# First norm, conditioning quarters and the order of the last product's chunks in a fused trunk step

## The chip, the cores and the metric

One core of one Trainium2 chip runs the whole kernel in one launch. The metric is device time in microseconds (us), as a median over runs; the profiled execution is one more run, taken with the profiler on. The engines are named as in the profile: PE multiplies matrices, DVE, ACT and POOL work element by element, SP only issues DMA transfers.

## The reference, cut to what matters

```python
# D_MODEL 1024; 1024 prompt tokens and 8 sequences x 8 sample tokens; DEPTH 1
sh, sc, gt = ada_mod(c, w_ada_mix, b_ada_mix)      # silu(c) @ w + b, split in three
h = rms_norm(x, norm_mix) * (1 + sc) + sh          # the start of the kernel
P = h @ w_in                                       # 30 column blocks of 128, K = 1024
...                                                # two branches, gates, w_out, residual
h = rms_norm(x, norm_mlp) * (1 + sc) + sh
x = x + gt * (square(relu(h @ w_ff1)) @ w_ff2)     # the last product
y = rms_norm(x, norm_final)                        # the end of the kernel
```

`rms_norm` divides each token by the root of the mean of its 1024 squares, and multiplies each feature by a weight. The conditioning vector c is one for the prompt and one for each of the eight sample sequences, so that shift, scale and gate have nine values for each feature.

## The kernel before, in words

Everything lies features first: a tensor of 1024 features and 1088 tokens (1024 prompt tokens, then 64 sample tokens) is eight row blocks `kb` of 128 features. Each product is done as three reduced-precision matmuls: every operand is split in a high part `hi` and a rest `lo`, and PE adds hi·hi, hi·lo and lo·hi (`mm3`, through `mm` at L148). A row block of h therefore is two tiles (the profile calls both `hx`), and a weight tile of 128x512 is loaded raw, copied to `whi` on ACT (L167) and subtracted to `wlo` on DVE or POOL (L168). The 1088 tokens are cut in three chunks of 364, 362 and 362.

The order on PE is the order in which the program is written: `Pace.run` weaves a main stream (the products) with side work by planned times. The order on the other engines is set by a scheduler from priorities and buffers.

**The start** (`start`, L342 to L410). SP loads the eight x rows (L359, 544 KB each); a small transfer on ACT's queue loads the sample columns of x once more into `smp` (L350), in pieces of 256 bytes. ACT squares each row (L362), DVE adds the squares up over the eight blocks (L366), and `stats` multiplies that sum by a column of ones, block of 128 tokens by block, so that the sums stand tokens first. `rms` (L281) takes the root on ACT, inverts on DVE, spreads the values back over 128 partitions by PE transposes (L155) and copies them to `rb` on ACT (L303). Meanwhile the conditioning weight `w_ada_mix` comes in two halves of eight tiles 128x1024 (L372); half i holds shift and scale for row blocks 4i to 4i+3. `ada_part` (L239) multiplies it in by column-tiled matmuls (eight rows of the trace for each turn of two tiles), copies the result (`asb`, L255), adds up the four column groups with a selection matrix (the eight rows `wc<-kct,asb`), adds the bias (`am`, L263), and `mod_scale` makes g (L268). Then for each row block: h = x·g·rb on DVE (L391), hi on ACT (L393), lo on DVE (L395). The sample columns go a separate way through `smp` on DVE (L386 to L388, L396). Row blocks 0 to 3 need the first half, 4 to 7 the second. The products of the first two column blocks of P start with row block 0 and go on as row blocks come; the second half's conditioning runs between them.

**The middle** is a long run of products with the recurrent branch beside it. Two small loads there are issued by SP: `plw` (L531) and the pool state (`spool`, L478).

**The end** (`last`, `norm3`, from about L1400). The last product runs through the tokens in three chunks `FCH`, of 448, 384 and 256 columns. For each of eight row blocks m, `residual` (L1448) adds the gated result to x on DVE (L1454); where the chunk holds the sample columns it needs one more DVE operation (L1457) and an addition on POOL (L1459). Squares on ACT (L1431), sums on DVE (L1433), `stats` and `rms` follow for each chunk, and then eight output rows: six on DVE (L1444), and in the last chunk two by POOL (L1441) and ACT (L1442). SP stores each row (L1445). The sample columns lie in the last chunk.

Of the kernel before, what the change touches and what calls it, by code (L numbers as in the profile page):

```python
# [18 lines left out]
P = 128  # L19
# [3 lines left out]
TS = 8  # L23
# [94 lines left out]
class K:  # L118
# [38 lines left out]
    def weights(self, src):  # L157
# [10 lines left out]
        (nc.gpsimd if n % 2 and n >= self.solo else nc.vector).tensor_tensor(lo, raw, hi.bitcast(F32), op=ALU.subtract)  # L168
# [112 lines left out]
    def rms(self, po, col, blocks, out):  # L281
# [7 lines left out]
        for i in range(0, k, 4):  # L289
            m = min(4, k - i)  # L290
            ps = self.ps("wc")
# [50 lines left out]
    def start(self, st, order):  # L342
# [4 lines left out]
        aw = lambda: st.tile([P, 1024], F32, tag="aw", bufs=8, name=self.nm("aw"))  # L347
        asb = st.tile([P, 512], F32, name="asb")
        smp = st.tile([P, 8, 64], F32, name="smp")
        nc.scalar.dma_start(smp, io["xT"][:, :, NPR:NT].rearrange("k p n -> p k n"))  # L350
        blocks = self.blocks(0, NT)
        po = self.ps("w")
        rt = self.cp.tile([P, 16], F32, tag="rt", bufs=2, name=self.nm("rt"))
        nc.scalar.activation(rt[:, 0:1], self.eps[:, 0:1], AF.Sqrt)
        xs = []
        t = None
        for kb in range(8):
            x = self.row(st, "x", 8)
            nc.sync.dma_start(x, io["xT"][kb])  # L359
            xs.append(x)  # L360
            sq = self.row(st, "sq", 3)
            nc.scalar.activation(sq, x, AF.Square)  # L362
            if t is None:
                t = sq
            else:
                nc.vector.tensor_tensor(t, t, sq, op=ALU.add)  # L366
        ws = []

        def load(i):
            for k in range(8):  # L370
                ws.append(aw())
                nc.sync.dma_start(ws[-1], io["w_ada_mix"][k, i])  # L372
# [3 lines left out]
        self.stats(po, t, blocks, True, True)  # L376
        rb = self.row(st, "rb", 1)
        pr, sa = slice(0, NPR), slice(NPR, NT)

        def part(i, gaps, turn):  # L380
            yield from self.ada_part("w_ada_mix", i, lambda: ws.pop(0), asb, self.am, "b_mix", (4 * i, 8 + 4 * i), gaps, turn)
            self.mod_scale(g, self.am, "norm_mix", 4 * i, 4 * i + 4)
            ks = slice(4 * i, 4 * i + 4)
            seq = lambda t: t[:, ks, 1:9].unsqueeze(3).to_broadcast([P, 4, 8, 8])
            s4 = smp[:, ks].rearrange("p k (q t) -> p k q t", t=TS)
# [15 lines left out]
        def rest():  # L401
            yield from part(1, (0, 0, 3000, 1500), 1500)
            self.done.add("h")
# [1174 lines left out]
```

## Time and profile before

| | |
|---|---|
| median of 3 runs | 1755.21 us (1754.6 to 1755.97) |
| profiled execution | 1759.32 us |
| its span on the core | 1757.5 us |
| PE busy | 1692.8 us (96%) |
| DVE / ACT / POOL busy | 845.0 / 546.1 / 255.1 us |
| mean granted TensorE clock | 0.984 |

The span runs from the first to the last instruction of the profiled execution; the times in the rows count from its start. A timeline row gives start, duration, engine, line, operation, output and inputs, shape, the number of instructions merged in the row, and in brackets how long the engine idled before and what released it. One fp32 matmul stands in the trace as two rows. Line numbers are those of the kernel before.

### The profile page before, as it was taken

Reading aid. Unit: us, or ns where it says so; the run is one execution under the profiler, and the core shown is the slowest. Engines: PE = TensorE matmul, PEld = TensorE weight load, DVE = VectorE, ACT = ScalarE, POOL = GpSimd, SP = SyncE. Lnnn points to the kernel's source line nnn. Section 1 sums busy time; section 2 is a strip of 40 time slices with the busy share of each in tenths; the row PEclk is TensorE's granted clock in tenths of the full one; section 3 lists DMA queues with packets and bytes.
Section 4 is the critical chain, followed back from the end, with each engine's and each line's share of the span. In section 5 each row is a group of like instructions: output and inputs, shape, how many; then the busy total and the mean of one; then the engine's idle time right before and its main releaser. Section 6 shows DMA issues by size and latency. Waiting matters only on the chain.

```text
span 1757.5 us, 32572 instructions
## 1 busy us (share of the span) xinstructions
PE 1692.8 (96%) x13705; PEld 1583.7 (90%) x13705; DVE 845.0 (48%) x1540; ACT 546.1 (31%) x1100; POOL 255.1 (15%) x335
## 2 busy tenths in 40 slices
PE   5999999999999999999999999999999999999997
PEld 2989878887888798899798999999999999999997
DVE  5577465746573744335437633323333333324346
ACT  4443343343343433322225521213121212212132
POOL 0120110000000000005314411111111111111111
PEclk9999999989999999999999999999999999999998
DMA  8233314222413241847842311111111111111112
GB/s 336 82 128 118 125 65 135 85 81 94 147 41 129 80 137 57 314 168 276 299 151 85 136 45 49 43 44 47 43 46 45 43 49 43 43 49 43 43 43 103
DMA packets 80083, 179.61 MB, mean 102 GB/s; under 512 B 16480, under 2 KB 23136, under 8 KB 79936
## 3 DMA queue, kind: packets, MB, share of 16 engines
q1 hardware_dynamic: 72128, 156.66, 26.0%
q10 hardware_dynamic: 6512, 15.96, 2.7%
q0 software_dynamic: 1296, 4.90, 0.7%
q8 instruction: 108, 1.77, 0.4%
q14 instruction: 39, 0.32, 0.1%
HBM read 138.64 MB, written 38.84 MB: 101 GB/s over the span
## 4 chain that ended last, share of the span: by engine, by line
PE 86%; DMA 4%; DVE 4%; ACT 2%; issue 2%; POOL 1%; SPq 0%; DVEq 0%; ACTq 0%; POOLq 0%
PE mm L148 58%; PE w L148 24%; PE wc L148 4%; DMA t<-d_th 1%; DMA smp<-in_xT 1%; PE w L155 1%; POOL t L1266 1%; DMA aw<-in_w_ada_mix 1%; DMA wraw<-in_w_in 1%; DMA hid<-in_w_ada_mlp 0%; ACT whi L167 0%; DVE hx L1444 0%; DMA wraw<-in_w_ff 0%; POOL wlo L168 0%; DVE wlo L168 0%
## 5 line engine op out<-in xcount | busy, mean ns | idle before, releaser
L148 PE MATMUL mm<-hx,whi 128*128 128x362 f32 (+2 forms) x2608 | 683.1, 344 | 2.6 <-ACT px L465 2.0
L148 PEld LDWEIGHTS mm<-hx,whi 128*128 128x128 f32 x2608 | 458.8, 191 | 39.6 <-issue 20.4
L148 PE MATMUL mm<-hx,wlo 128*128 128x362 f32 (+3 forms) x1304 | 430.7, 330 | 1.8 <-DVE wlo L168 1.8
L167 ACT ACTIVATE whi<-wraw 128x512 fp32r<-128x512 f32 x246 | 155.1, 630 | 531.4 <-PE w L148 359.1
L148 PE MATMUL mm<-ma,whi 128*128 128x364 f32 (+1 forms) x1280 | 318.0, 330 | 0.2 <-ACT whi L167 0.2
L148 PEld LDWEIGHTS mm<-hx,wlo 128*128 128x128 f32 x1304 | 249.9, 192 | 2.3 <-DVE wlo L168 2.1
L148 PEld LDWEIGHTS mm<-ma,whi 128*128 128x128 f32 x1280 | 226.7, 189 | 7.3 <-issue 5.0
L168 POOL TENSOR_TENSOR wlo<-wraw,whi 128x512 fp32r<-128x512 f32 x89 | 117.6, 1322 | 670.4 <-ACT whi L167 670.4
L168 DVE TENSOR_TENSOR wlo<-wraw,whi 128x512 fp32r<-128x512 f32 x157 | 110.4, 704 | 211.6 <-ACT whi L167 211.3
L148 PE MATMUL mm<-ma,wlo 128*128 128x364 f32 (+1 forms) x640 | 210.4, 329 | 0.1
L1454 DVE SCALAR_TENSOR_TENSOR hx<-mm,aq,hx 128x364 f32<-128x364 f32 (+4 forms) x136 | 74.8, 588 | 207.8 <-PE mm L148 207.5
L148 PE MATMUL w<-mb,whi 128*128 128x362 f32 x640 | 159.1, 330 | 2.5 <-DVE rs L1457 2.1
L148 PEld LDWEIGHTS mm<-ma,wlo 128*128 128x128 f32 x640 | 120.6, 189 | 0.4 <-DVE wlo L168 0.4
L148 PEld LDWEIGHTS w<-mb,whi 128*128 128x128 f32 x640 | 112.7, 189 | 5.9 <-issue 4.4
L1349 DVE TENSOR_TENSOR ft<-ft 128x362 f32<-128x362 f32 (+1 forms) x96 | 53.1, 577 | 131.5 <-ACT ft L1348 131.2
L148 PE MATMUL w<-mb,wlo 128*128 128x362 f32 x320 | 105.5, 330 | 0.8 <-DVE wlo L168 0.8
L148 PE MATMUL w<-hx,whi 128*128 128x362 f32 x416 | 103.2, 329 | 0.1
L148 PE MATMUL mm<-hid,whi 128*128 128x364 f32 (+4 forms) x304 | 75.0, 328 | 0.0
L148 PEld LDWEIGHTS w<-hx,whi 128*128 128x128 f32 x416 | 73.7, 190 | 0.4 <-DVE hx L396 0.4
L1348 ACT ACTIVATE ft<-mm 128x364 f32<-128x364 f32 x64 | 29.5, 475 | 124.9 <-PE mm L148 124.7
L148 PE MATMUL w<-hx,wlo 128*128 128x362 f32 x208 | 67.8, 326 | 0.0
L1459 POOL TENSOR_TENSOR hx<-hx,rs 128x64 f32<-128x64 f32 x72 | 38.6, 537 | 176.8 <-DVE rs L1457 176.6
(309 smaller groups left out, 2120.8 us busy)
## 6 DMA issues: line engine op xcount, KB each, us to landing
wraw<-in_w_ff SPq DMA_DIRECT2D x134, 256.0 KB, 2.6
wraw<-in_w_in SPq DMA_DIRECT2D x68, 256.0 KB, 2.8
hid<-in_w_ada_mlp SPq DMA_DIRECT2D x24, 512.0 KB, 4.8
d_th<-px SPq DMA_DIRECT2D x22, 544.0 KB, 3.0
wt<-d_x SPq DMA_DIRECT2D x20, 544.0 KB, 4.4
t<-d_th ACTq DMA_DIRECT2D x16, 544.0 KB, 5.7
aw<-in_w_ada_mix SPq DMA_DIRECT2D x16, 512.0 KB, 7.2
wraw<-in_w_out SPq DMA_DIRECT2D x32, 256.0 KB, 2.9
```

The costliest lines, as they stand in the source:

```text
L148: return self.nc.tensor.matmul(out, lhsT, rhs, **kw)
L155: self.nc.tensor.transpose(out, in_, ident)
L167: nc.scalar.activation(hi, raw, AF.Copy)
L168: (nc.gpsimd if n % 2 and n >= self.solo else nc.vector).tensor_tensor(lo, raw, hi.bitcast(F32), op=ALU.subtract)
L1266: nc.gpsimd.tensor_tensor(t, t, S["u"], op=ALU.add)
L1348: nc.scalar.activation(t[:, :n], ps[:, :n], AF.Relu)
L1349: nc.vector.tensor_tensor(t[:, :n], t[:, :n], t[:, :n], op=ALU.mult)
L1454: nc.vector.scalar_tensor_tensor(x[:, c0:c0 + m], ps[:, :m], gt[:, 0:1], x[:, c0:c0 + m], op0=ALU.mult, op1=ALU.add)
L1459: nc.gpsimd.tensor_tensor(x[:, NPR:NT], x[:, NPR:NT], t, op=ALU.add)
```

## The change

**First norm.** The squares of row blocks 0-2, 3-5 and 6-7 are added up on DVE as three groups. PE multiplies each group by a 128x128 matrix of ones, in three parts of 512, 512 and 64 tokens, which leaves the sum over all features on every partition. The root is taken from there; a 32x32 transposing on DVE, a reciprocal of one value per token, and a transposing of the spread value give `rb`. `stats`, `rms` and the load of `smp` are no longer used at the start. **Conditioning.** `w_ada_mix` is loaded in quarters, each two tiles of [128, 2, 4, 256] by two transfers each, with runs of 1 KB; quarter qi holds shift and scale for row blocks 2qi and 2qi+1. The first rows are made in three chunk pieces. The sample columns are made in place in x, on POOL. The first two `wlo` are made on POOL. **Loads.** `plw` and the pool state are issued from POOL. **End.** `FCH` is reversed, so that the sample columns lie in the first chunk; six of eight output rows of the middle chunk (`late`) are put behind the last residual, with a copy `nf` of the norm's weights that POOL makes from there; six rows of the last chunk read the spread values directly from PSUM.

```diff
+                if kb % 3:
+                    nc.vector.tensor_tensor(ts[-1][:, s], ts[-1][:, s], sq[:, s], op=ALU.add)
+            if kb % 3 == 0:
+                ts.append(sq)
+            if kb in (2, 5, 7):
+                for s, ps in zip(parts, pss):
+                    self.mm(ps[:, :s.stop - s.start], ones, ts[-1][:, s], start=kb == 2, stop=kb == 7)
...
+            for r in range(2):
+                w = st.tile([P, 2, 4, 256], F32, tag="aw", bufs=5, name=self.nm("aw"))
+                for s in range(2):
+                    o = s * 512 + qi % 2 * 256
+                    nc.sync.dma_start(w[:, s], io["w_ada_mix"][4 * r:4 * r + 4, qi // 2, :, o:o + 256].rearrange("k p c -> p k c"))
...
+            nc.scalar.activation(rb[:, s], ps[:, :n], AF.Sqrt, bias=self.eps[:, 0:1], scale=1.0 / D)
+            nc.vector.transpose(rt1[:, s], rb[:, s])
+            nc.vector.reciprocal(rr[:, c], cut32(rt1)[:, c, 0])
+            nc.vector.transpose(cut32(rb)[:, c, :], rr[:, c].unsqueeze(2).to_broadcast([P, n // 32, 32]))
...
+                xq = cut8(x[:, sa])
+                nc.gpsimd.tensor_tensor(xq, xq, g[:, kb, 1:9].unsqueeze(2).to_broadcast([P, 8, 8]), op=ALU.mult)
+                nc.gpsimd.tensor_tensor(x[:, sa], x[:, sa], rb[:, sa], op=ALU.mult)
+                nc.gpsimd.tensor_tensor(xq, xq, self.am[:, kb, 1:9].unsqueeze(2).to_broadcast([P, 8, 8]), op=ALU.add)
+                nc.scalar.activation(hi[:, sa], x[:, sa], AF.Copy)
+                nc.gpsimd.tensor_tensor(lo[:, sa], x[:, sa], hi[:, sa].bitcast(F32), op=ALU.subtract)
...
+                    late = [] if ci == 0 else [lambda m=m, out=out, r=rb[:, c0:c0 + n]: out(m, r) for m in range(2, 8)]
+                    for m in range(8 if ci == 0 else 2):
+                        out(m, rb[:, c0:c0 + n], ci == 1)
+                else:
+                    for m in (7, 6, 0, 1, 2, 3, 4, 5):
+                        out(m, rb[:, c0:c0 + n] if m > 5 else self.rps[:, :n], m > 5)
...
-FCH = [(0, 448), (448, 384), (832, 256)]
+FCH = [(640, 448), (256, 384), (0, 256)]
```

PE at the start, before: from the last transpose of the norm through the selection (`wc_292`) and the second half's first turns (`wc_342`) to the first products (`mm_354`, `w_355` are the first column block).

```order
13 L155 MATMUL wc_289<-kct,rt_261 128x128
14 L148 MATMUL wc_292<-kct,asb 128x18 x4
15 L148 MATMUL wc_342<-aw_326,sT 32x512 x2
16 L148 MATMUL wc_342<-aw_328,sT 32x512 x2
17 L148 MATMUL wc_342<-aw_330,sT 32x512 x2
18 L148 MATMUL wc_342<-aw_332,sT 32x512 x2
19 L148 MATMUL mm_354<-hx_147,whi_236 128x364
20 L148 MATMUL mm_354<-hx_148,whi_236 128x364
21 L148 MATMUL mm_354<-hx_147,wlo_237 128x364
```

PE at the start, after: the last of the ones products (`sq_218,ones`), quarter 0 (`wc_271`), its selection, and the first products.

```order
8 L148 MATMUL mm_180<-sq_218,ones 128x512
9 L148 MATMUL mm_181<-sq_218,ones 128x64
10 L148 MATMUL wc_271<-aw_232,sT 32x512 x4
11 L148 MATMUL wc_271<-aw_235,sT 32x512 x4
12 L148 MATMUL wc_282<-sel_173,asb_280 128x9 x4
13 L148 MATMUL mm_334<-hx_147,whi_240 128x364
14 L148 MATMUL mm_334<-hx_148,whi_240 128x364
15 L148 MATMUL mm_334<-hx_147,wlo_241 128x364
```

The half and its first turns of the next half ahead of the products are now one quarter; six turns (of four matmuls each) and three selections of the later quarters stand among the products of row blocks 0 to 4, where two turns and one selection stood.

DVE between the second quarter's selection and the lo parts of its rows, after (`hx_152` and `hx_154` are the lo parts of row blocks 2 and 3).

```order
35 L414 TENSOR_TENSOR am<-wc_372,part 128x2x18 [waits PE_49]
36 L268 SCALAR_TENSOR_TENSOR g_172<-am,part 128x18 [waits DVE_49]
37 L422 SCALAR_TENSOR_TENSOR h_379<-x_191,g_172,sq_256 128x1024 [waits DMAHW3_49,DVE_49]
38 L422 SCALAR_TENSOR_TENSOR h_388<-x_199,g_172,sq_256 128x1024 [waits DMAHW4_49]
39 L424 SCALAR_TENSOR_TENSOR hx_152<-h_379,am,hx_151 128x1024 [waits Activation_49]
40 L424 SCALAR_TENSOR_TENSOR hx_154<-h_388,am,hx_153 128x1024 [waits Activation_49]
```

Before, row blocks 2 and 3 had no selection of their own: their h stood behind the lo parts of row blocks 0 and 1.

```order
24 L395 SCALAR_TENSOR_TENSOR hx_148<-h_302,am,hx_147 128x1024 [waits Activation_49]
25 L395 SCALAR_TENSOR_TENSOR hx_150<-h_308,am,hx_149 128x1024 [waits Activation_49]
26 L396 TENSOR_TENSOR hx_148<-smp,hx_147 128x64 [waits Activation_49]
27 L396 TENSOR_TENSOR hx_150<-smp,hx_149 128x64 [waits Activation_49]
28 L391 SCALAR_TENSOR_TENSOR h_314<-x_188,g_172,rb_255 128x1024 [waits DMAHW4_49,DVE_49]
29 L391 SCALAR_TENSOR_TENSOR h_320<-x_193,g_172,rb_255 128x1024 [waits DMAHW5_49,DVE_49]
```

So a selection and two vector operations now stand ahead of every second row block.

DVE at the end, before, from the last residual (L1454) to the last output rows (L1444).

```order
1513 L1454 SCALAR_TENSOR_TENSOR hx_9168<-mm_17044,aq,hx_9168 128x192 [waits PE_49]
1514 L1457 TENSOR_TENSOR rs_17041<-mm_17024,aq 128x64 [waits Pool_49]
1515 L1457 TENSOR_TENSOR rs_17061<-mm_17044,aq 128x64 [waits Pool_49]
1516 L1433 TENSOR_TENSOR t_16983<-t_16983,t_17008 128x256 [waits Activation_49]
1517 L1433 TENSOR_TENSOR t_16983<-t_16983,t_17028 128x256 [waits DVE_49,Activation_49]
1518 L1433 TENSOR_TENSOR t_16983<-t_16983,t_17048 128x256 [waits DVE_49,Activation_49]
1519 L287 RECIPROCAL rt_17070<-rt_17070 128x2 [waits Activation_49]
1520 L1444 SCALAR_TENSOR_TENSOR hx_8703<-hx_8703,part,t_16572 128x256 [waits Activation_49]
```

DVE at the end, after, at the same place (`nf` rows are the middle chunk's late ones, `wc_17123` is the PSUM with the spread values).

```order
1512 L1479 TENSOR_TENSOR t_17031<-t_17031,t_17087 128x256 [waits DVE_49,Activation_49]
1513 L1515 SCALAR_TENSOR_TENSOR hx_9213<-mm_17083,aq,hx_9213 128x256 [waits PE_49]
1514 L1496 SCALAR_TENSOR_TENSOR hx_8876<-hx_8876,nf,t_16617 128x384 [waits Pool_49]
...
1519 L1496 SCALAR_TENSOR_TENSOR hx_9213<-hx_9213,nf,t_16617 128x384
1520 L287 RECIPROCAL rt_17120<-rt_17120 128x2 [waits Activation_49]
1521 L1496 SCALAR_TENSOR_TENSOR hx_8748<-hx_8748,part,wc_17123 128x256 [waits Activation_49]
```

The six late rows stand between the last residual and the reciprocal, and the sample operations are gone from there.

## Rows read from the trace of the kernel before

**Rows 1.** Windows: length, busy us (instructions) of PE, PEld, DVE, ACT, POOL; clock; DMA.

```profile
58.00:60.00 2.00, 2.00 (x9) 2.00 (x8) 2.00 (x3) 1.03 (x1) 0.00 (x0) 0.50 0.42 156
...
1000.00:1690.00 690.00, 690.00 (x4167) 686.79 (x4166) 244.11 (x459) 150.23 (x292) 102.28 (x114) 1.00 0.15 48
```

**Rows 2.** The chain that ended last, in order of time: its first two long pieces.

```profile
1.19 14.74 DMA smp<-in_xT
16.32 4.61 DMA aw<-in_w_ada_mix
```

**Rows 3.** Timeline of all engines from 0 to 39 us.

```profile
15.95 4.22 SPq L372 DMA_DIRECT2D aw<-in_w_ada_mix  x8
...
22.93 1.93 PE L148 MATMUL wc<-aw,sT 128*32 128x512 f32 x8
...
31.68 0.58 ACT L255 ACTIVATE asb<-wc 128x512 f32<-128x512 f32 x1
...
32.31 1.07 PE L148 MATMUL wc<-kct,asb 128*128 128x18 f32 x8 [1.22 <-ACT asb L255]
...
33.42 0.23 DVE L263 TENSOR_TENSOR am<-wc,part 128x72 f32<-128x72 f32 x1 [0.19 <-PE wc L148]
...
34.26 2.47 DVE L391 SCALAR_TENSOR_TENSOR h<-x,g,rb 128x1024 f32<-128x1024 f32 x2
...
36.99 2.47 DVE L395 SCALAR_TENSOR_TENSOR hx<-h,am,hx 128x1024 fp32r<-128x1024 f32 x2
```

**Rows 4.** Timeline of PE from 38 to 70 us.

```profile
38.59 0.33 PE L148 MATMUL mm<-hx,wlo 128*128 128x364 f32 x1
...
41.67 1.06 PE L148 MATMUL wc<-aw,sT 128*32 128x512 f32 x8
...
56.10 0.44 PE L148 MATMUL mm<-hx,wlo 128*128 128x364 f32 x1 [1.83 <-DVE wlo L168]
...
68.90 0.50 PE L148 MATMUL mm<-hx,whi 128*128 128x362 f32 x2
69.23 0.33 PE L148 MATMUL mm<-hx,wlo 128*128 128x362 f32 x1
```

**Rows 5.** DMA from 0 to 60 us: GB/s by 1.5 us, and queues (packets, MB, share of 16 engines).

```profile
GB/s 0 143 393 384 416 411 410 412 413 415 68 202 401 281 344 391 426 415 406 349 357 410 421 403 422 418 412 314 16 0 0 0 0 0 0 0 5 0 273 77
...
q1 hardware_dynamic: 5504, 14.55, 63.8%
q10 hardware_dynamic: 1184, 0.30, 2.3%
```

**Rows 6.** Groups on DVE and POOL by line and shape: busy us, mean ns.

```profile
L773 DVE STREAM_TRANSPOSE hv<-iv 128x512 f32<-128x512 f32 x4 | 4.8, 1197 | 1.3 <-ACT iv L770 1.3
...
L428 POOL COPY px<-sst 128x8 f32<-128x8 f32 x14 | 3.2, 235 | 5.9 <-DMA sst<-in_sst 5.8
```

**Rows 7.** Durations of L1459 on POOL, in ns: smallest, median, largest.

```profile
L1459 POOL TENSOR_TENSOR hx<-hx,rs x72: 311/378/2032, 933.9 to 1745.7; 128x64 f32<-128x64 f32 x72
```

**Rows 8.** Timeline of all engines from 67.5 to 71 us.

```profile
69.26 1.29 DVE L444 TENSOR_TENSOR d<-px 128x1096 f32<-128x1096 f32 x1
69.33 1.28 POOL L441 COPY ns<-px 128x8 f32<-128x8 f32 x1
```

**Rows 9.** Timeline of all engines from 1738 us to the end.

```profile
1738.70 4.33 DVE L1444 SCALAR_TENSOR_TENSOR hx<-hx,part,t 128x384 f32<-128x384 f32 x8
...
1742.92 0.87 PE L148 MATMUL mm<-hx,ma 128*128 128x256 f32 x6
...
1746.66 1.86 PE L148 MATMUL wc<-kct,t 128*128 128x2 f32 x8 [2.87 <-DVE t L1433]
...
1750.28 3.40 DVE L1444 SCALAR_TENSOR_TENSOR hx<-hx,part,t 128x256 f32<-128x256 f32 x6 [1.26 <-ACT t L303]
...
1750.39 1.82 POOL L1441 TENSOR_TENSOR hx<-hx,t 128x256 f32<-128x256 f32 x2 [4.16 <-ACT t L303]
```

**Rows 10.** Timeline of SP's queue from 1749 us: the last stores.

```profile
1750.83 4.14 SPq L1445 DMA_DIRECT2D o_y<-hx  x8
```

More of the change, by code (lines that the diff above doesn't have):

```diff
@@ L279, in stats, with rms @@
             self.mm(po[:, i:i + m], t[:, b:b + 128], self.kc("one0")[:, :m], start=first and i == 0, stop=last and i == len(blocks) - 1)
-    def rms(self, po, col, blocks, out):
+    def rms(self, po, col, blocks, out, tag="wc"):
         nc = self.nc
@@ L346, in start @@
         g = self.cp.tile([P, 8, 9], F32, name="g1")
[L347 to L352, printed above, removed]
+        sel = st.tile([P, 9], F32, name="sel4")
+        nc.gpsimd.tensor_tensor(sel, self.kc("sel")[:, 0:9], self.kc("sel")[:, 9:18], op=ALU.add)
+        ones = st.tile([P, P], F32, name="ones")
+        nc.gpsimd.memset(ones, 1.0)
         rt = self.cp.tile([P, 16], F32, tag="rt", bufs=2, name=self.nm("rt"))
-        nc.scalar.activation(rt[:, 0:1], self.eps[:, 0:1], AF.Sqrt)
-        xs = []
-        t = None
+        nc.scalar.activation(rt[:, 0:1], self.sT[:, 0, 0:1], AF.Sqrt, bias=self.eps[:, 0:1], scale=0.0)
+        parts = (slice(0, 512), slice(512, 1024), slice(1024, NT))
+        pss = [self.ps("mm") for _ in parts]
+        xs, ts = [], []
         for kb in range(8):
@@ L360, in start @@
             xs.append(x)
[L361 to L366, printed above, removed]
-        ws = []
[L369 to L372, printed above, removed]
+            sq = self.row(st, "sq", 4)
+            for s in parts if kb == 7 else (slice(0, NT),):
+                nc.scalar.activation(sq[:, s], x[:, s], AF.Square)
+                if kb % 3:
+                    nc.vector.tensor_tensor(ts[-1][:, s], ts[-1][:, s], sq[:, s], op=ALU.add)
@@ L398, in start @@
-        self.pace.run(iter(()), [part(0, (0, 3500, 0, 0), 1000), self.rms(po, 0, blocks, rb)])
-        load(1)
-        def rest():
-            yield from part(1, (0, 0, 3000, 1500), 1500)
+        load(1)
+        rb, rt1, rr = self.row(st, "sq", 4), self.row(st, "sq", 4), st.tile([P, 34], F32, name="rr")
+        for s, ps in zip(parts, pss):
+            n = s.stop - s.start
+            nc.scalar.activation(rb[:, s], ps[:, :n], AF.Sqrt, bias=self.eps[:, 0:1], scale=1.0 / D)
+            nc.vector.transpose(rt1[:, s], rb[:, s])
+            c = slice(s.start // 32, s.stop // 32)
+            nc.vector.reciprocal(rr[:, c], cut32(rt1)[:, c, 0])
+            nc.vector.transpose(cut32(rb)[:, c, :], rr[:, c].unsqueeze(2).to_broadcast([P, n // 32, 32]))
@@ L403, in rest @@
+        for r in range(2):
+            round_(0, r)
+        for _ in vectors(0, 0):
+            pass
+        rows(0)
+        load(2)
+        load(3)
+        def rest():
+            for qi in range(1, 4):
+                yield (1000, 3000, 2500)[qi - 1]
+                round_(qi, 0)
+                yield (600, 700, 1600)[qi - 1]
+                round_(qi, 1)
+                yield from vectors(qi, 1100)
+                rows(qi)
             self.done.add("h")
```

69 lines of the change are left out of this document (43 added, 26 removed).

## The prediction

> **What bounds the kernel now.** I read the windows first. From 1000 to 1690 us PE is busy in 690.00 of 690 us at a granted clock of 1.00 [rows 1], and the change leaves the order there as it was. So only the two ends, where PE waits, can give or take time. At the front the chain starts with the transfer of the sample columns, which lands at 15.93 us, and goes on with the conditioning weights [rows 2]. SP issues the weights at 15.95, just behind that landing [rows 3], and the DMA rate falls from 415 GB/s to 68 and 202 GB/s in the two slices from 15 to 18 us [rows 5]. The first vectors wait for 4.2 MB of weights: `asb` starts at 31.68 and h at 34.26 [rows 3]. The first product with a lo part starts one matmul (0.17 us) before the row at 38.59, at 38.4; the last product of the first two column blocks ends at 69.23 plus half of its row, 69.4 [rows 4]. The stretch takes 31.0 us. At the tail the last residual's products end at T = 1743.79, and the last of eight stores is issued at 1754.97, T + 11.2 [rows 9, 10].
>
> **Start, up to the first rows.** Without the sample transfer the weights follow x at once, from about 14.2 us: the full-rate slices end at 15.0 [rows 5], and the sample packets leave them. Their price: queue 10 moved 1184 packets in 2.3% of 16 x 60 us, 18.6 ns each of 256 bytes; queue 1 moved 5504 in 63.8%, 111 ns each of 2.64 KB [rows 5]. A straight line through both gives 8.7 ns and 0.0388 ns a byte, so 168 ns for a 4 KB run (what the kernel before uses) and 48 ns for 1 KB. The first quarter, 2.1 MB in runs of 1 KB, takes 2048 x 48 / 16 = 6.2 us and lands at 20.4; in 4 KB runs it would take 5.4. The smaller runs cost 0.8 us there (bounds 0 and 1.5, the line being drawn through mixed queues).
>
> [...] The rows here have 256 byte packets at 18.6 ns, more than twice their share.
>
> Behind the landing stand one turn on PE (1.0 us, half of 1.93 [rows 3]), the copy of the first whi ahead of `asb` on ACT, and then `asb` to h as before: 34.26 - 31.68, less a sample operation of 0.4 that now runs on POOL, 2.2 us [rows 3]. That puts h at 24.2. The norm is ready earlier. The last square ends at about 16.2; the nine ones products are 18 trace rows, of which the last group's end at 18.9; then come a root, and on DVE four transposes of 512 columns at up to 1.2 us [rows 6], and rb is whole at 23.7. If a transpose from a spread value cost twice that, rb would be last, at 25 to 26: the bound on that side.
>
> Six h pieces follow, at 2.47/2 for 1024 columns or 0.46 a piece, 2.75 us, then a lo piece of 0.5 [rows 3]: 27.5 us. Beside them POOL now makes the sample columns, six operations of 128x64 before their hi parts. Rows of POOL and DVE side by side show what that can cost: a POOL copy of 128x8 took 1.28 us beside a DVE operation of 1.29 [rows 8], where the same copy has a mean of 0.235 [rows 6]; and the six last rows on DVE took 3.40 us, 0.57 each for 256 columns [rows 9], where eight of 384 columns took 4.33, 0.54 each. So either side can be held. Six POOL operations at 0.311, the smallest, to 0.378, the median [rows 7], would hold DVE by 0 to 2.3 us; I take 0.9, about 0.15 each, as in those six rows. The first product with a lo part then stands at 28.4, **10 us earlier**.
>
> **Start, to the end of the two column blocks.** Most of it is given back. PE's work from there was 144 matmuls at 0.166 us [rows 4], two turns at 1.06 and a selection at 1.0, 27.0 us; the rest of 31.0 was a stall of 1.83 and the slow matmuls behind it [rows 4]. Now six turns and three selections stand in it: 23.9 + 6.4 + 3.0 = 33.3 us. What had hidden them, the time before the first rows, is gone. And each quarter's chain, from selection to first lo, stands on DVE with am and g (0.5), two h (1.2 each) and a lo (1.25), 4.2 us and up to 4.5 beside POOL, while PE has between 3.0 and 4.5 us of products left. Going through the order after, the stalls are 1.6 us at row block 2, 1.7 at 4 (two wlo stand there too) and 0.9 at 6, together 4.2; without POOL's hold 1.9. The stretch takes 37.5 us (35.2 without).
>
> **The clock.** Before the first rows PE now has almost nothing from 23.7 to 28.4 us. The row for that: after the idle 1.83 us at 56.10 [rows 4] the granted clock was 0.50, that is 1.2 GHz, from 58 to 60 [rows 1], and matmuls took twice as long for about 3 us, 1.7 us lost. I charge 1.9 (bounds 0 and 3). Sum: 28.4 + 37.5 + 1.9 = 67.8 against 69.4, a **gain of 1.6 us**.
>
> **Tail.** Before, eight middle rows of 4.33 us sit in front of the last residuals, and the sample operations on DVE and POOL lie between the last product and the stats at 1746.66 [rows 9]. After, two middle rows go by POOL, six wait behind the last residual. Residual at T + 0.1 to T + 0.5, square to T + 1.0, stats of 1.86 us [rows 9] from T + 1.5, of which the first half can run early, root to T + 3.6 at the latest. DVE is in the six late rows until T + 4.3 (from T + 1.0, behind `nf` on POOL, 6 x 0.54); reciprocal and spread to T + 5.2; rows from T + 5.25 at 0.41 each, since they read PSUM. Eight stores of 4.14 us [rows 10] then bound it: T + 9.9 against T + 11.2. **Gain 1.3 us** (0.5 to 2.3; the six late rows are what eats the rest).
>
> [...]
>
> **The middle** I take as 0 (±0.5): `plw` and the pool state are issued from POOL, which has gaps there, ahead of where they are used. Together 1.6 + 1.3 = 2.9 us; the profiled execution would go from 1759.3 to 1756.4, and the median from 1755.21 to **1752.4**.
>
> **The rivals.**
> First, the forecast, with the early start mostly given back: 0.44. Its own range is 1750 to 1754.5.
> Second, PE stays fed: POOL holds DVE little (27.5), the stretch takes 35.2, and with the same clock price the blocks end at 64.6, 4.8 earlier; with the tail 6.1, 1749.1. With a clock that holds it would be 1747. For it: DVE operations that did not suffer beside POOL, as the 1.29 us one [rows 8]. Against: the chains of 4.2 us, which do not depend on POOL. 0.30.
> Third, the slower side: the clock falls at each quarter. The mechanism is the 1.83 us stall at 56.10, after which PE ran at 1.2 GHz [rows 1, 4]. Its place is the waits for the first lo of row blocks 2, 4 and 6, its price 1.7 us each, 5.1 together, plus up to 3.4 where POOL holds DVE by 2.3 us (1.4 more in the first quarter, 2 in the others). It decides from the point where these stalls reach that 1.83 us; mine are 1.6, 1.7 and 0.9. The start then loses 3.5 to 6.9, the tail gives 1.3: +2.2 to +5.6, 1757.4 to 1760.8. 0.19, of which 0.12 over the slower bound.
> Fourth, that the change does not do what it says: the conditioning still comes late (runs of 1 KB at the rate of the 256 byte packets, 2048 x 74 / 16 = 9.5 us, and rb late too), rows at 27, and the start comes out even. The tail alone gives 1754. 0.07.
>
> **How the numbers follow.** A measurement of this kernel can tell 0.2%, 3.5 us, from no change: bounds 1751.7 and 1758.7. Of the forecast a third (0.14) falls under the lower bound, the rest within; the second rival is faster (0.30), the third slower by 0.12 and the same by 0.07, the fourth the same. Faster 0.44, same 0.44, slower 0.12. The range from 1746.5 to 1758.7 leaves out the best of the second (0.07) and the 0.12 of the third.
>
> **What would show it.** Right: the weights issued before 6 us or on x's heels, no gap in the DMA rate at 15 us; h at 24 to 25 us; the first lo product at 27.5 to 28.5; PE waits for lo of row blocks 2, 4 and 6 of 1 to 2 us; the first block pair ending near 68; a granted clock of 0.5 for some 3 us at the first products; last stores at T + 9.5 to T + 10.5. Wrong: PE without waits at the quarters and an end near 64 (second rival); a granted clock of 0.5 again after each quarter (third); h later than 26.5 (fourth); or middle products that shifted, since I priced them at nothing.

## The result, and the profile after

The changed kernel takes 1762.91 us (median of 10 runs, 1757.99 to 1768.07) against 1754.55 us for the kernel before, measured beside it: ratio 1.0046, interval 1.0032 to 1.0060. A second comparison later (e16 below) gave 1.0029, interval 1.0017 to 1.0040. The mean of the two is some 1.0037, or 6.5 us slower. I had forecast 2.9 us faster, and the range ended at 1758.7.

The page of the changed kernel opens with the span and the busy times: PE is busy 2.7 us longer than before, and the profiled execution is 4 us longer than the one of before (1761.5 against 1757.5). That is less than the medians differ: the profiled execution of the kernel before (1759.32 us) was 4.8 us slower than its median beside the changed kernel, that of the changed kernel (1763.26) only 0.35.

```profile
span 1761.5 us, 32639 instructions
PE 1695.5 (96%) x13712; PEld 1583.4 (90%) x13712; DVE 843.6 (48%) x1542; ACT 548.5 (31%) x1108; POOL 285.6 (16%) x383
```

I cut both spans at the same two points: the end of the first two column blocks, and T, the end of the last residual's products. Before: 69.4 us of start [rows 4], 1674.3 of middle (to T = 1743.8 [rows 9]) and 13.7 of tail. After: 69.5, 1679.4 and 12.6. So **the start came out even, the tail gave what it should, and the middle, which I had priced at 0, lost 5 us**.

**Start.** The DMA rates by 1.5 us answer to [rows 5]; the gap at 15 us is gone, and the quarters with runs of 1 KB come at some 348 GB/s.

```profile
GB/s 0 155 375 414 415 363 267 403 415 409 370 348 350 348 364 368 347 348 349 348 348 349 350 348 348 366 365 354 90 8 0 0 0 0 0 7 168 0 5 168
```

The timeline of the start (columns as in [rows 3]) has the ones products, the transposing, the first vectors, the first rows, and in the last row the end of the two column blocks: the last of their products runs into the row that starts at 69.35.

```profile
5.30 9.23 SPq L378 DMA_DIRECT2D aw<-in_w_ada_mix  x4
...
11.44 4.08 PE L148 MATMUL mm<-sq,ones 128*128 128x512 f32 x6 [11.44 <-DVE sq L364]
...
16.36 6.28 PE L148 MATMUL mm<-sq,ones 128*128 128x512 f32 x12 [0.85 <-DVE sq L364]
...
22.37 0.71 DVE L389 STREAM_TRANSPOSE sq<-sq 128x512 f32<-128x512 f32 x1 [3.71 <-ACT sq L387]
...
22.57 1.92 PE L148 MATMUL wc<-aw,sT 128*32 128x512 f32 x16
...
24.56 0.60 ACT L407 ACTIVATE asb<-wc 128x512 f32<-128x512 f32 x1 [0.64 <-PE wc L148]
...
27.09 3.39 DVE L422 SCALAR_TENSOR_TENSOR h<-x,g,sq 128x364 f32<-128x364 f32 x6
...
31.10 0.67 PE L148 MATMUL mm<-hx,whi 128*128 128x364 f32 x1 [1.92 <-DVE hx L424]
...
69.35 0.32 PE L148 MATMUL mm<-hx,wlo 128*128 128x362 f32 x1
```

h starts at 27.09 (before 34.26 [rows 3]) and the first lo product at 31.10 (its row is the one with 1.92 us of waiting). PE's waits between the first rows and 70 us, from its timeline; in brackets how long, and for whom:

```profile
43.32 0.44 PE L148 MATMUL mm<-hx,whi 128*128 128x364 f32 x1 [0.89 <-DVE hx L424]
54.26 0.43 PE L148 MATMUL mm<-hx,whi 128*128 128x364 f32 x1 [0.26 <-DVE hx L424]
57.80 0.43 PE L148 MATMUL mm<-hx,wlo 128*128 128x364 f32 x1 [0.41 <-DVE wlo L168]
63.48 0.44 PE L148 MATMUL mm<-hx,whi 128*128 128x364 f32 x1 [0.23 <-DVE hx L424]
```

Two windows of the same kernel (the granted clock is the third number from the end): 0.50 while the first rows come, and 1.00 from 58 to 60 us, where [rows 1] had 0.50. The prediction writes this 0.50 as 1.2 GHz; the profile gives the clock as a share of full speed alone. At 0.50 three products of 362 columns took 0.90 us (from 31.88 on), 1.2 columns a ns.

```profile
28.00:34.00 6.00, 3.57 (x13) 2.78 (x17) 5.52 (x11) 3.25 (x8) 3.23 (x6) 0.50 1.10 348
...
58.00:60.00 2.00, 2.00 (x16) 2.00 (x16) 0.87 (x3) 0.00 (x0) 0.46 (x2) 1.00 0.36 126
```

**Tail.** Rows that answer to [rows 9, 10]. T is 1748.04 + 0.87 = 1748.9; the sixteen stores are issued by 1758.84, T + 9.9; the six late rows start at T + 1.1, and the last six, which read PSUM, take 0.41 us each (0.57 before).

```profile
1745.56 13.28 SPq L1497 DMA_DIRECT2D o_y<-hx  x16
...
1748.04 0.87 PE L148 MATMUL mm<-hx,ma 128*128 128x256 f32 x6
...
1749.97 3.26 DVE L1496 SCALAR_TENSOR_TENSOR hx<-hx,nf,t 128x384 f32<-128x384 f32 x6 [0.54 <-POOL nf L1485]
...
1753.16 0.15 DVE L287 RECIPROCAL rt<-rt 128x2 f32<-128x2 f32 x1
...
1754.57 2.44 DVE L1496 SCALAR_TENSOR_TENSOR hx<-hx,part,wc 128x256 f32<-128x256 f32 x6 [1.26 <-ACT t L303]
```

**Middle.** From 70 us to T, PE's idle time is 36.0 us, against 29.8 before. Nearly all of it lies ahead of 1000 us in both. Two rows of PE's timeline after have no counterpart before:

```profile
197.21 0.60 PE L148 MATMUL mm<-hx,whi 128*128 128x362 f32 x2 [1.78 <-issue]
...
547.25 1.96 PE L148 MATMUL w<-ab,at 64*64 64x128 f32 x32 [1.67 <-ACT at L893]
```

In the first, PE waits for nothing that the profile shows. In the second it waits for a copy `at` on ACT. ACT's timeline after shows why: the two scalings of `wt`, which wait 5.93 us for a load, stand ahead of the copies `at` and `uv`.

```profile
545.18 1.39 ACT L606 ACTIVATE wt<-wt,part 128x512 f32<-128x512 f32 x2 [5.93 <-DMA wt<-d_x]
546.60 0.60 ACT L893 ACTIVATE at<-w 128x512 f32<-128x512 f32 x1
547.09 0.58 ACT L895 ACTIVATE uv<-w 64x512 f32<-64x512 f32 x1
```

Before, the copies stood first, and no line of the diff names any of them. ACT and PE there:

```profile
544.79 0.60 ACT L848 ACTIVATE at<-w 128x512 f32<-128x512 f32 x1 [3.57 <-PE w L148]
545.56 0.59 ACT L850 ACTIVATE uv<-w 64x512 f32<-64x512 f32 x1 [0.17 <-DVE uv L849]
547.16 1.39 ACT L561 ACTIVATE wt<-wt,part 128x512 f32<-128x512 f32 x2 [1.01 <-DMA wt<-d_x]
```

```profile
547.40 1.97 PE L148 MATMUL w<-ab,at 64*64 64x128 f32 x32
```

These two waits are real, but they are not where this pair of traces parts. The product behind the second one starts at 547.25 after and at 547.40 before, so that the two traces are level there, and they still are at 709 us. From 70 to 547 us PE was busy 3.0 us longer before (461.0 against 458.1), at a mean granted clock of 0.97 against 0.98, and idled as much less. The 5 us come between 709 us and 1000 us, where PE of the changed kernel idled 2.2 us more and had the lower clock, first after and then before:

```profile
700.00:1000.00 300.00, 287.80 (x2082) 265.60 (x2083) 143.64 (x232) 98.81 (x176) 90.76 (x85) 0.98 0.56 197
```

```profile
700.00:1000.00 300.00, 289.98 (x2123) 265.77 (x2122) 147.73 (x238) 100.84 (x180) 91.11 (x86) 1.00 0.57 200
```

One pair of executions can't tell which part of that belongs to the kernel and which to the run; the medians of the experiments below have to.

### The profile page after: what moved, and what is told of

It is laid out like the page before. It is cut to its first block, busy times and chain, and to the rows that moved or that the text cites. A ratio compares the mean times of both kernels' runs of the same rounds, so it can differ in the third digit from the quotient of the medians.

```text
span 1761.5 us, 32639 instructions
## 1 busy us (share of the span) xinstructions
PE 1695.5 (96%) x13712; PEld 1583.4 (90%) x13712; DVE 843.6 (48%) x1542; ACT 548.5 (31%) x1108; POOL 285.6 (16%) x383
## 3 DMA queue, kind: packets, MB, share of 16 engines
q8 instruction: 108, 1.77, 0.4%
## 4 chain that ended last, share of the span: by engine, by line
PE 85%; DVE 5%; DMA 4%; ACT 2%; issue 2%; POOL 1%; SPq 0%; ACTq 0%; DVEq 0%; POOLq 0%
PE mm L148 57%; PE w L148 24%; PE wc L148 3%; DMA t<-d_th 2%; PE w L155 1%; DMA wt<-d_x 1%; DVE h L422 0%; DMA wraw<-in_w_in 0%; POOL t L1311 0%; DMA hid<-in_w_ada_mlp 0%; DMA x<-in_xT 0%; DMA wraw<-in_w_out 0%; DVE wlo L168 0%; SPq L378 0%; ACT whi L167 0%
## 5 line engine op out<-in xcount | busy, mean ns | idle before, releaser
L1515 DVE SCALAR_TENSOR_TENSOR hx<-mm,aq,hx 128x364 f32<-128x364 f32 (+3 forms) x136 | 75.1, 588 | 206.3 <-PE mm L148 206.2
```

Of the source, the lines that this page charges most:

```text
L1515: nc.vector.scalar_tensor_tensor(x[:, c0:c0 + m], ps[:, :m], gt[:, 0:1], x[:, c0:c0 + m], op0=ALU.mult, op1=ALU.add)
```

## The experiments

Ratios are to the kernel before, with a 95% interval; the kernel before had medians of 1755.1 to 1756.6 us beside them. The letters of the theories in the expectations hold within one group of runs: e1 to e4, e5 to e8, e9 to e12, e13 to e16. A difference of 0.001 is 1.75 us.

### The parts of the change apart

e1 is the changed kernel with the two small loads issued by SP again:

```diff
-            nc.gpsimd.dma_start(ev[:, :, 0:15], self.io["spool"][:, g])
+            nc.sync.dma_start(ev[:, :, 0:15], self.io["spool"][:, g])
-            nc.gpsimd.dma_start(plw, self.io["pool_w"][:, g * 128:(g + 1) * 128])
+            nc.sync.dma_start(plw, self.io["pool_w"][:, g * 128:(g + 1) * 128])
```

> The changed kernel with the two small loads (plw and the pool state) issued from SP again, as in the kernel before. In the traces the two column blocks end at 69.5 us against 69.4, the tail gives 1.1 us, and the middle loses 5.1 us, of which 1.7 stand at 545.6 us, where ACT takes a scaling that waits for a DMA ahead of the copy that PE needs; with the loads on SP that swap is gone from the order. Theory A (the loads on POOL cost the middle, by that swap and by POOL's queue): some 4 to 5 us less than the changed kernel, about 1758, ratio 1.002. Theory B (any shift of the start moves the middle's transfers against its products, and the loads have no part in it): as the changed kernel, 1761 to 1763, ratio 1.0045.

e2 is the kernel before with only those two loads moved to POOL (the same lines the other way).

> The kernel before with nothing changed but the two small loads, issued from POOL. Theory A: 3 to 5 us slower than before, ratio 1.002 to 1.003. Theory B: no change, within 0.1%. Its order on PE, DVE and ACT is that of the kernel before, without the swap on ACT, so that only the queue's own price is seen.

e3 has the new start, with the loads on SP and the tail of the kernel before; e4 is the kernel before with the new tail only. Beside the late rows, the line that goes back in e3 and forth in e4 is

```diff
-FCH = [(0, 448), (448, 384), (832, 256)]
+FCH = [(640, 448), (256, 384), (0, 256)]
```

> The changed kernel with the old end (chunks of 448, 384, 256 from the front, old order of rows) and the loads on SP: the first norm and the conditioning alone. From the traces the two column blocks end 0.1 us later than before, so by Theory A: within 1 us of the kernel before, ratio 1.000. Theory B: the whole loss is here, 7 to 9 us, ratio 1.004 to 1.005.

> The kernel before with the new order of the last product's chunks and rows alone. All theories but one: 1.1 us faster, as the tails of the two traces differ, ratio 0.9994. A third theory (the new chunk order costs in the last product, ahead of the tail): slower, by 2 us or more.

Measured: e1 1759.6 us, 1.0018 (1.0005 to 1.0030); e2 1756.91, 1.0003 (0.9992 to 1.0014); e3 1759.48, 1.0020 (1.0008 to 1.0032); e4 1756.78, 0.9999 (0.9988 to 1.0010). Neither the tail nor the two loads alone cost anything. The new start costs 0.2% by itself. And taking the loads from POOL in the changed kernel gave back a part (by the first result; against e16 the intervals overlap). That had a reason besides the loads: the order on ACT is the old one in e1. Its rows there:

```profile
540.88 0.60 ACT L893 ACTIVATE at<-w 128x512 f32<-128x512 f32 x1 [3.62 <-PE w L148]
541.65 0.59 ACT L895 ACTIVATE uv<-w 64x512 f32<-64x512 f32 x1 [0.17 <-DVE uv L894]
542.68 1.39 ACT L606 ACTIVATE wt<-wt,part 128x512 f32<-128x512 f32 x2 [0.44 <-DMA wt<-d_x]
```

The load is the same, the scaling waits 0.44 us for it, and PE does not wait. So e1 against the changed kernel mixes two things, which e13 and e14 take apart.

### The clock held at the start

e5 is e1 with five unread fp32 products that keep PE busy while the first rows come: one of 512 columns ahead of the first turn, two behind the selection, two behind the first hi·hi (where `mm3` calls `fill` once).

```diff
+        dummy = self.ps("w")
+        def fill(k, n):
+            for _ in range(k):
+                nc.tensor.matmul(dummy[:, :n], ones, xs[0][:, :n], start=True, stop=True)
+        fill(1, 512)
...
+        fill(2, 512)
+        self.fill = fill
```

> The kernel of e1 (loads on SP) with five matmuls added whose result nobody reads, in the waits of PE between the ones products and the first products: one ahead of the first turn, two behind the selection, two behind the first hi·hi; everything else in the same order. Over all runs the mean granted clock of e1 and e3 was 0.983 to 0.984 against 0.986 of the kernel before, and at an equal clock their spans do not differ; in the traces 10.2 us at half clock lie around the first products (25.6 to 35.8) where the kernel before has 0 to 7. Theory C (the new start costs by the clock that falls in PE's waits before the first products): the clock stays at full there, the block pair ends 1 us or more earlier, mean clock back to 0.985 to 0.986, and 2 to 3 us faster than e1, about 1757. Theory D (the clock that is lost is lost elsewhere, or the first products wait for DVE anyway): as e1, 1759 to 1760, with the mean clock still near 0.983.

e6 adds a sixth, of 256 columns, ahead of the selection; with it the order on ACT is that of the changed kernel.

```diff
+            if qi == 0:
+                fill(1, 256)
```

> As e5, with a sixth such matmul (256 columns) ahead of the selection. With it the scheduler puts two scaling operations (wt), which wait for a DMA, ahead of two copies (at, uv) on ACT in the middle of the program, as it does in the changed kernel; nothing else differs from e5. Theory A1 (this swap on ACT is what the loads on POOL cost the changed kernel): 2 to 3 us slower than e5, with a wait of PE of some 1.7 us at 545 us, ahead of a product of ab and at. Theory A2 (POOL's queue itself costs): as e5, within 1 us.

Measured: e5 1759.17 us, 1.0020 (1.0007 to 1.0033); e6 1759.85, 1.0029 (1.0017 to 1.0040). The same window as above, first e1 and then e5:

```profile
28.00:34.00 6.00, 4.18 (x16) 2.52 (x16) 4.22 (x9) 2.09 (x6) 1.94 (x4) 0.50 1.14 313
```

```profile
28.00:34.00 6.00, 5.55 (x31) 2.38 (x29) 4.48 (x9) 2.35 (x6) 2.19 (x5) 1.00 1.14 313
```

The granted clock is 1.00 in that window of e5 (0.50 in e1), and its two column blocks end at 67.1 instead of 69.5. So the low clock at the start is real and worth 2.3 us there. Yet the whole kernel is no faster: the medians of e5 and e1 differ by 0.4 us, so that some 2 us of the gain went elsewhere. The profile of e5 has a middle 8.8 us longer than that of e1, but most of that is the choice of the execution: e5's profiled one is 3.1 us over its median, e1's is the fastest of its twelve and 3.5 us under it. It is a first hint, not more, that moving instructions costs something later on.

### The start cut out

e7 and e8 leave out all that follows the first four column blocks (outputs are then filled from loaded data); e7 has the start of before, e8 that of e1.

```diff
-        jobs += G[8:]
+        jobs = [X(0), X(8)]
...
-        self.pace.run(back, [self.chains(), self.heads(), self.pools(), self.or_rows()])
+        self.pace.run(back, [])
```

> The kernel before, cut: the start and the first four column blocks of P only; the rest of the program is left out, and the outputs are copies of one row. Its time, 110 to 130 us, is the price of the start without the noise of the rest. To be compared with e8 alone.

> The changed start (loads on SP), cut in the same way as e7. If the start itself costs the 3 us that e3 showed: 2 to 4 us slower than e7 in the medians. If the start is even, as the traces have it (block pairs end at 69.3 to 69.4 against 69.1 to 72.1): within 1 us of e7, or up to 2 us faster, and the 3 us come from the middle.

Measured: e8 121.3 to 122.4 us in four runs, mean 122.0; e7 123.08 and 124.08 us, and 126.28 and 126.35 in two more runs at a lower mean clock than the first two (0.879 against 0.891 and 0.897). The new start is 1.6 us faster by the first two, which was the forecast for it, and 3.0 by all four; so few runs that differ by 3 us are a thin base. In the profiles of the changed kernel and of the kernel before it is even.

### TensorE's instructions moved against their pieces

I took queue 8, of kind "instruction", for the one that brings PE's code. Its row on the changed kernel's page:

```profile
q8 instruction: 108, 1.77, 0.4%
```

1.77 MB in 108 packets is 16.4 KB each. The page has 2 x 13712 PE and PEld instructions; if the queue is PE's that is 64.5 bytes for each, so about 256 in a piece. That it is PE's, e15 below bears out: with 256 more PE instructions, its page shows one piece more.

```profile
q8 instruction: 109, 1.79, 0.4%
```

Around 190 us, in a burst of 32x32 products, the pieces come every 4 us. Up to the product near 195 us the traces hold 2987 instructions of PE before (matmuls, weight loads and semaphore instructions), 3010 in the changed kernel and in e1, 3009 in e3, 3031 in e5; the expectation of e11 counts to an earlier place, with the same difference of 23. The wait "issue" near 195 us is there in all of those with the higher counts, and not in before, e2 and e4. So I moved PE's instructions without touching the rest: unread products of 32x32, four PE instructions each, early in the start. The lines of e9 (6 of them, in the kernel before):

```diff
+        dummy = self.ps("w")
+        for _ in range(6):
+            nc.tensor.matmul(dummy[0:32, :32], self.kct[0:32, 0:32], self.kct[0:32, 0:32], start=True, stop=True)
```

e10 has 11, e11 is e1 with 58 (so that 23 + 232 = 255 makes a whole piece), e12 is e5 with 53.

> The kernel before with six 32x32 matmuls added whose result nobody reads, early, where PE idles; the order on all engines is else the same. They are 24 instructions of PE. In the traces PE's program comes in by 16 KB pieces on queue 8 (108 pieces for 1.77 MB, so 256 instructions of 64 bytes each), and PE stands without a named cause (issue) for 1.2 to 1.8 us at 192 to 197 us in the changed kernel, e1, e5 and e6, behind some 250 tiny matmuls, and not in the kernel before; up to there the changed kernel has 23 instructions of PE more than the kernel before, e5 45 more. Theory F (where the pieces begin in the program sets these waits, and the added instructions of the new start have shifted them): 1 to 3 us slower than the kernel before, with a wait at 195 us as in the changed kernel. Theory G (the shift has no part in it): as the kernel before.

> As e9 with eleven such matmuls, 44 instructions, the shift of e5. Theory F: 1 to 3 us slower than the kernel before, with a wait of 1.8 us within the tiny matmuls at 192 us, as in e5. Theory G: as the kernel before.

> The kernel of e1 (new start and end, loads on SP) with 58 such matmuls ahead of the ones products: with them the program of PE stands to the 16 KB pieces as in the kernel before (2860 instructions and 232 more, less the 2837 of the kernel before, is 255, one piece). Theory F: the wait at 195 us goes, and 1 to 3 us of the 3 that e1 lost come back: 1756 to 1758. Theory G: as e1, 1759 to 1760.

> The kernel of e5 (clock held up before the first products) with 53 such matmuls, so that PE's program stands to the pieces as in the kernel before. Theory F: the wait at 192 us goes with the fall of the clock behind it, and with the block pair at 67 us and the end's 1.1 us it is 2 to 4 us faster than the kernel before, 1753 to 1755. Theory G: as e5, 1759.

Measured: e9 1759.44 us, 1.0017 (1.0005 to 1.0030); e10 1761.29, 1.0025 (1.0013 to 1.0037); e11 1758.35, 1.0006 (0.9994 to 1.0019); e12 1757.27, 1.0002 (0.9989 to 1.0015). Six unread products, 0.84 us of PE's idle time at 8.6 us, make the kernel before as slow as e1. Fifty-eight of them in e1 make it no slower, rather faster, though the intervals of the two overlap. The row of e10:

```profile
194.81 0.24 PE L148 MATMUL w<-hv,iv 32*32 32x32 f32 x2 [1.56 <-issue]
```

e11 and e12 have no such row there.

### The two causes apart in the changed kernel

e13 and e14 are the changed kernel, loads on POOL and all, with 58 and 60 such products. With 58 the order on ACT is the old one, with 60 it is the changed kernel's (the first `asb` copy also changes places with its neighbour there, and PE's shift is 7 past a whole piece). Apart from those two scalings, the operations of ACT, DVE and POOL between 100 and 1600 us stand in one order in the traces of before, the changed kernel, e1, e5, e6, e9, e13, e14 and e15, so that no other swap is a rival there. e15 is the control: the kernel before with 64, a whole piece. e16 is the changed kernel again.

```diff
+        pad = self.ps("w")
+        for _ in range(58):
+            nc.tensor.matmul(pad[0:32, :32], self.kct[0:32, 0:32], self.kct[0:32, 0:32], start=True, stop=True)
```

> The changed kernel as it stands, loads on POOL included, with 58 unread fp32 products of 32x32 ahead of the first norm: 232 TensorE instructions, which with the 23 more of the change make 255, so that the middle's instructions stand against the 16 KB pieces (256 instructions of 64 bytes) as in the kernel before. ACT's order around the wt scaling is that of e1 and of the kernel before. Theory F+G (fetch position and ACT order make the loss): 1.0005 (1756.5 to 1758.5), like e11; no issue stall of PE near 197 us and no wait of 1.67 us for ACT near 545 us. Theory L (loads on POOL): 1.002 or more (over 1759.5), since they are kept. If the start's lower clock makes the loss: 1.0025 or more.

> As e13 with 60 such products (263 instructions in all, 7 past a whole piece), with which ACT keeps the changed kernel's order: the wt scaling ahead of the copies of at and uv. Theory G (ACT's order costs some 2 us): 1.2 to 2.5 us over e13, ratio 1.0015, and the wait of PE near 545 us is there again, 1.3 to 1.7 us. Theory F alone: as e13 within 0.7 us. Theory L: as e13.

> The kernel before with 64 such unread products at the place where e9 had 6 and e10 had 11: 256 TensorE instructions, one whole 16 KB piece. Theory F: the piece boundaries fall again where they fell, so it is at 1.0000 to 1.0010 (1756.3 to 1758), below e9 and e10 although it does six to ten times their extra work; no issue stall near 195 us. If the extra instructions themselves cost what e9 and e10 lost: over 1.0025, 1761 or more.

> The changed kernel once more, for the comparison on one chip: 1.0035 to 1.0055 (1762.5 to 1766), clock near 0.983, with the issue stall near 197 us and the wait for ACT near 545 us, if both come from the order of the program and not from chance. If the first result was a matter of the chip: below 1.0025.

Measured: e13 1759.59 us, 1.0017 (1.0005 to 1.0029); e14 1763.31, 1.0040 (1.0026 to 1.0054); e15 1756.61, 1.0011 (1.0001 to 1.0022); e16 1761.51, 1.0029 (1.0017 to 1.0040).

The order on ACT: e14 is 3.7 us slower than e13 (by the means of the runs 4.1, with a standard error of 1.0). ACT and PE in e14,

```profile
549.91 1.39 ACT L609 ACTIVATE wt<-wt,part 128x512 f32<-128x512 f32 x2 [5.62 <-DMA wt<-d_x]
551.33 0.60 ACT L896 ACTIVATE at<-w 128x512 f32<-128x512 f32 x1
```

```profile
551.98 1.96 PE L148 MATMUL w<-ab,at 64*64 64x128 f32 x32 [1.23 <-ACT at L896]
```

and ACT in e13, where PE has no such wait:

```profile
540.75 0.60 ACT L896 ACTIVATE at<-w 128x512 f32<-128x512 f32 x1 [3.92 <-PE w L148]
541.53 0.59 ACT L898 ACTIVATE uv<-w 64x512 f32<-64x512 f32 x1 [0.17 <-DVE uv L897]
542.42 1.39 ACT L609 ACTIVATE wt<-wt,part 128x512 f32<-128x512 f32 x2 [0.31 <-DMA wt<-d_x]
```

The wait seen is 1.0 to 1.7 us in the four traces that have it (1.67 in the changed kernel, 0.96 in e16, 1.33 in e6, 1.23 in e14); the rest of the 3.7 is within what the intervals allow.

The position: e15 has ten times the extra work of e9 and comes out lower, with no issue wait near 195 us, as expected of a whole piece. But its interval overlaps those of e9 and e10. The issue wait is there again in e16 and gone in e13 and e14. For all that e14 is no faster than the changed kernel, and e13 at 1.0017 missed the 1.0005 expected of it. A part of that is the control itself: with the new start the many products are not free. In e14

```profile
8.74 6.60 PE L356 MATMUL w<-kct 32*32 32x32 f32 x120 [8.74 <-DMA kct<-in_kc]
```

they hold PE up to 15.3 us, where the ones products had started at 11.4 in the changed kernel, and the two column blocks end at 71.0 in e14, 70.9 in e13 and 71.5 in e11, against 69.5 in the changed kernel and e1. So these three pay 1.4 to 2.0 us at the start, by one trace each, and a gain of that size further on does not show in their ratios. e15 pays nothing there (68.5 against 69.4).

PE's idle time, by stretches of the profiles, points the same way. From 70 to 330 us it is 6.5 to 7.7 us in the eight kernels that have the issue wait and 5.5 to 5.9 in the eight that have not (e16 counted by itself). From 330 to 700 us it is 15.0 to 16.1 in the four with the wt scaling first and 13.0 to 14.5 in the others. From 700 to 1000 us it runs from 6.8 to 10.0 in the seven with neither and from 8.6 to 12.7 in the nine with one or both; what the two have to do with that last stretch is not shown.

By groups, put together after the runs (means of the ratios):

| PE instructions, order on ACT | kernels | mean ratio |
|---|---|---|
| as before, as before | e2, e4 | 1.0001 |
| moved by 255 to 257, as before | e11, e12, e13, e15 | 1.0009 |
| moved by 23 to 45, as before | e1, e3, e5, e9, e10 | 1.0020 |
| any, wt scaling first | after, e6, e14, e16 | 1.0036 |

No kernel of the third group lies below any of the second (e9 and e13 are equal), and none of the fourth below any of the third. None of the fourteen full kernels beats the kernel before.

## Why the prediction was wrong

**The step that failed** is the sentence "The middle I take as 0 (±0.5)", and ahead of it "only the two ends, where PE waits, can give or take time". It measured +5.1 us in the pair of profiles. It rested on the windows, in which 690 us of the middle are dense and stay so, and on the two loads, which indeed cost nothing that can be measured alone (e2). What I left out is that a changed start also changes the middle's surroundings: PE's instruction stream is 23 longer ahead of it, and the scheduler put two scalings on ACT ahead of two copies, 475 us behind the end of the edited start. The text named it as what would make it wrong, "middle products that shifted, since I priced them at nothing". The order of ACT's instructions is known before a kernel runs, and the swap stands in it; I argued from the order at the two ends alone. Nearly all of PE's idle time in the middle, some 30 us, lies between 70 and 1000 us, and [rows 1] shows no window of that stretch.

Sizes, from the runs: the order on ACT 1.6 us (e6 against e5, whose intervals overlap widely; the medians differ by 0.7) to 3.7 us (e14 against e13, whose intervals overlap by 0.0003); the wait of 1.0 to 1.7 us that it makes is in the rows of every kernel that has it and of no other. The position of PE's instructions 1.1 to 3.2 us (e9 and e10 against e15, e1 against e11, e5 against e12), borne out by the groups and the row at 195 us, but with overlapping intervals in each pair, and nothing in the pair of e14 and the changed kernel, where the start of e14 hides 1.5 us. Together with a start that was 1.7 us worse than forecast, that covers 4.4 to 8.6 of the 9.4 us between forecast and result. What the loads on POOL add when the rest has changed too (e13 against e11, 0.0011) stays open, and so does how the parts add up: with two causes of 2 us and intervals of 2 us either way, I can't settle the sum. That both act is shown; that they make up the whole loss is not, least of all in the one pair of profiles, which parts behind both of them.

**Start, up to the first rows**: late by 2.7 us. The rate of the 1 KB runs was sized well (348 GB/s against 338 in the sum). Against the slices of 403 to 426 in [rows 5] it makes the 1 KB runs 16 to 22% dearer, where the line through the rows had 14% (four of 48 ns against 168). One reading there was off: 18.6 ns for 256 bytes is 1.7 times their share of 111 ns for 2.64 KB, not "more than twice". The transposes took 0.67 to 0.84 us, under the bound of 1.2. Two terms were mis-sized. One is "the last group's end at 18.9": the ones products ended at 22.64, and the first turn stands behind them on PE, so that `asb` started at 24.56 and not at 22.0. The other is that the first quarter "lands at 20.4". In e1, with the same start, the ones products ended at 19.8, and there the second turn waited for the weights:

```profile
21.97 1.07 PE L148 MATMUL wc<-aw,sT 128*32 128x512 f32 x8 [1.19 <-DMA aw<-in_w_ada_mix]
```

so that `asb` started at 23.09; in e16 the same turn waited until 22.97. Of the 2.6 us by which `asb` was late, some 1.1 would have come from the weights alone. Then h took 0.565 us a piece, a little under the 0.61 of the sum (0.46 and 0.15 of hold).

**POOL's hold on DVE** was over-sized: 0.6 us in the first quarter, not 0.9, and in the second quarter the pair of h took 2.66 us against 2.47, and it was POOL's operations that took longer:

```profile
39.34 2.66 DVE L422 SCALAR_TENSOR_TENSOR h<-x,g,sq 128x1024 f32<-128x1024 f32 x2
39.38 1.54 POOL L426 TENSOR_TENSOR x<-x,g 128x64 f32<-128x64 f32 x2 [8.15 <-DVE g L268]
40.88 2.56 POOL L427 TENSOR_TENSOR x<-x,sq 128x64 f32<-128x64 f32 x2
```

POOL's last two took 1.28 us each, for an operation of 0.378 [rows 7]. Its first two took 1.54 together, so that no more than one of them can have been as long. What decides which of the two engines is held is not shown.

**The stretch** was 38.4 us against 37.5 + 1.9. The stalls at the quarters were 0.9, 0.7 and 0.2 us, together 1.8, not 4.2. The clock made up for it: a granted clock of 0.50 for 6.8 us, where I had some 3. The sum was nearly right with two terms wrong in opposite ways.

**The tail** was right but for one step: late rows from T + 1.1 (T + 1.0 in the text), the reciprocal at T + 4.3, PSUM rows at 0.41 us, last store at T + 9.9; only the last rows started at T + 5.7 and not at T + 5.25. The span ends 1.1 us sooner behind T, forecast 1.3. In e4 that is too little to be seen in the medians.

**The rivals.** The second (PE stays fed) fell with the late rows. The third had the right sign and the wrong place: the granted clock did not fall at the quarters, where the stalls were 0.9, 0.7 and 0.2 us; from 36 to 69.5 us it was 1.00. The fourth has its signs: h came at 27.09, past its mark of 26.5, the weights and rb (whole at 25.7, not 23.7) were late, and the start came out even. Its reason was another: the runs of 1 KB came at 348 GB/s, not at the 9.5 us a quarter that it named. Its time (1754) fell with the middle.

## What to carry to other kernels

An edit at one end of a scheduled kernel is not priced until the instruction order of every engine has been compared over the whole length: two operations that change places far away can cost more than the edit gains (here 1.6 to 3.7 us, against a forecast gain of 2.9). Look for an operation that waits for a load and now stands ahead of one that PE needs. And where some 2 us are at stake, add a control that moves the instructions and nothing else, before a gain or a loss is put down to the edit.

## What the runs showed of the hardware

**24 PE instructions whose result nobody reads, placed in idle time, cost 0.17%** (e9; interval 0.05 to 0.30), and 44 cost 0.25% (e10; 0.13 to 0.37), while 256 cost 0.11% (e15; 0.01 to 0.22). The last interval overlaps the other two, so the times alone don't show that the loss doesn't grow with the work; the wait near 195 us points to it, which is there in e9 and e10 and gone in e15. It is 0.7 to 1.8 us in the kernels that have it, and the profile names no releaser for it.

**A window of the profile reads 1.00 where the trace has no record of the clock.** In the changed kernel the eighteen rows of the ones products took 4.08 + 6.28 us, and in e1 the same eighteen took

```profile
11.79 8.00 PE L148 MATMUL mm<-sq,ones 128*128 128x512 f32 x18 [11.79 <-DVE sq L364]
```

The window from 16 to 19 us reads 1.00 in the changed kernel:

```profile
16.00:19.00 3.00, 2.64 (x3) 1.17 (x4) 1.74 (x4) 1.60 (x4) 0.00 (x0) 1.00 1.10 352
```

But the trace holds no clock record ahead of 20.8 us there (15.4 in e1), and the weight loads of these products change at that time: they took 0.34 us and stood 0.85 apart up to 19.94, and 0.19 and 0.43 apart from 21.02.

```profile
19.08 0.34 PEld L148 LDWEIGHTS mm<-sq,ones 128*128 128x128 f32 x1 [0.52 <-issue]
21.45 0.19 PEld L148 LDWEIGHTS mm<-sq,ones 128*128 128x128 f32 x1 [0.24 <-issue]
```

A pace near half is also what 0.50 gives where it is on record: three products took 0.90 us from 31.88 on, and 0.50 us from 66.04 on with 1.00 granted. So PE ran slowly up to some 20 us in that execution, which made the ones products end late, and only the durations tell it.

**Mean clock and time go together from run to run.** The 12 runs of e1 go from 1756.06 us to 1763.06 us, at mean granted clocks of 0.985 and 0.979. The means of the kernels: 0.986 for before, 0.983 for the changed kernel and e1, 0.985 for e5, where PE was kept busy at the start. So the new start goes with a lower mean clock, and keeping PE busy gives most of it back. The time does not follow: e5 is as slow as e1.
